# Half-K order for the last six output-projection chunks, with operand tiles reused for the block forms

## The chip, the cores and the metric

The kernel runs as one program on one core of a Trainium2 chip. The metric is the device time of one execution in microseconds (us), taken as the median of several runs. The engines are named as in the profile: PE (matmul), PEld (its weight loads), DVE (vector), ACT (scalar), POOL (GpSimd) and SP (which issues most DMAs).

## What is computed

One encoder layer in float32 on 512 tokens of width 2048. A mixing part (retention heads and state-space heads) ends in an output projection that is added to the residual; then come a gated MLP of inner width 5632 with a width-3 convolution on its gate, a gated per-layer input, and a last norm.

```python
h = h + jnp.concatenate([ret, ssd], axis=-1) @ w_out[i]
hn = rmsnorm(h, norm_ffn_w[i])
h = h + conv_glu_ffn(hn, ffn_w_gate[i], ffn_w_up[i], ffn_conv_w[i], ffn_conv_b[i], ffn_w_down[i])
gate = jax.nn.sigmoid(rmsnorm(h, ple_norm_w[i]) @ ple_w_gate[i] + ple_b_gate[i])
h = h + gate * (p[i] @ ple_w_proj[i])
return rmsnorm(h, final_norm_w)
```

## The kernel before, in words

Activations lie transposed: features on the 128 partitions, the 512 tokens along the row. A float32 product is made of three matmuls in the chip's fp32r type (`mm3`, L263): each operand is split into a high part (cast by ACT) and a low part (the rest, subtracted on DVE), and hi·hi, hi·lo and lo·hi are summed in PSUM. A weight unit is 128x1024 elements (512 KB), loaded by SP into one of four `raw` buffers and split into `whi` (L246, ACT) and `wlo` (L247, DVE), two units ahead of their use.

**Output projection** (L963 to 983). Sixteen chunks of 128 output features, in the order 0, 8, 1, 9, ... For each, `gemm_chunk` runs 16 steps of K with moving operands of 512 columns (`xh0..15`, `xl0..15`, the 64 KB pool `op` on the left side of SBUF). Then DVE adds the residual (`hc`, L969), ACT squares it for the norm (`sq`), POOL adds the squares up (`ssq`, L373), the chunk is stored to DRAM, and ACT writes it, times the norm weight, into `xw` (L978).

**MLP input** (L1009 to 1055, 44 chunks of the inner width). Gate and up projection are computed together by a seven-product block scheme. Input features pair up: chunk j with chunk j+8, eight pairs. For each pair there are seven operand forms of 256 tokens, high and low: `Eh{j}`, `El{j}` (`form_tiles`). Three forms are blocks of `xw` (`singles`), four are sums and differences of them (`sums`). A form costs DVE a subtraction for the low part (L932) and ACT a cast (L931), and the sums cost DVE five more adds of 256 columns per pair. One product (`prod`) runs over the eight pairs in the order j = 0 to 7, three matmuls of 256 columns each, 24 in all; a chunk has seven products, 168 matmuls. The weight forms are made the same way by `weight_form`.

Pairs 0 to 2 (`EARLY = 3`) are made during the output projection, in a pool on the right side. Pairs 3 to 7 lie in a pool on the left (`fb`) that takes the place of `op`; it opens only after the last output chunk, when `op` is closed. The norm (`token_norm`: 8 matmul records of one column, `rstd`, POOL's power, two diagonal tiles, two broadcast matmuls, copy into `Rb`) has its stages called in chunk 0 behind the first and second product, but a scheduler places instructions by priority and waits, so the order on each engine differs from the text.

**MLP output and gate.** Six groups of `acts` chunks, `ah`/`al`, lie alternately on the right (groups 0, 2, 4) and on the left (1, 3, 5) of SBUF. The per-layer gate uses sixteen operand pairs in `op2`, on the right. In the program as built, every operand tile on the right starts 32 bytes past a multiple of 64 bytes; the operand tiles of the same products on the left start on a multiple of 64.

Of the kernel before, what the change touches and what calls it, by code (L numbers as in the profile page):

```python
# [60 lines left out]
EARLY = 3  # L61
# [26 lines left out]
def layer(ctx: ExitStack, tc: tile.TileContext, xT, pT, pos, w_xbc, w_v, w_z, w_q, w_k, w_g,  # L88
# [11 lines left out]
    rope = mix.enter_context(tc.tile_pool(name="rope", bufs=1))  # L100
    ps = ctx.enter_context(tc.tile_pool(name="ps", bufs=4, space=PSUM))
# [227 lines left out]
    def diag_tokens(r, pool, tag=None):  # L329
# [4 lines left out]
        dh = pool.tile([P, NB, P], F32R, name=tag or "bc_dh", bufs=2 if tag else 1)[:, 0:nb]  # L334
        dl = pool.tile([P, NB, P], F32R, name=tag or "bc_dl", bufs=2 if tag else 1)[:, 0:nb]
# [620 lines left out]
    fa = ExitStack()  # L956
    fa_p = fa.enter_context(tc.tile_pool(name="fa", bufs=1, side="right", reuse_waits="tile"))
# [346 lines left out]
```

## Time and profile before

| what | us |
|---|---|
| median of 3 runs (2540.93 to 2545.3) | 2542.1 |
| the profiled execution, whole | 2543.66 |
| its span, first to last instruction | 2541.9 |
| PE busy in it | 2464.6 |
| mean granted clock of PE | 0.985 |

The profile has one execution. Its page shows busy time by engine, the span in 40 slices, the chain of work that ended last, the costliest groups of instructions and the DMA issues; the trace answers questions on a stretch, a line or a tile. Matmuls are pipelined: a record of a 512-column matmul lasts 0.39 us although the next starts 0.23 us later, so starts, not durations, are compared. 1.00 of granted clock is 2.4 GHz, 0.50 is 1.2 GHz.

### The profile page before, as it was taken

What the parts mean: (1) busy time and instruction counts of PE and PEld (TensorE: products, weight loads), DVE (VectorE), ACT (ScalarE), POOL (GpSimd) and SP (SyncE); (2) the same over time, 40 slices, a digit from 0 to 9 for tenths busy, and PEclk for the clock granted to TensorE, in tenths of its full rate; (3) what the DMA queues carried; (4) which work ended last, traced back from release to release, by engine and by line L of the source; (5) the groups of instructions that cost most, each with busy time, mean ns of one, the idle gap of its engine ahead of it and who ended that gap; (6) DMA issues with size and microseconds to landing.
All of it is one profiled execution on the core that took longest, in us unless ns stands there. A gap on an engine that the chain in (4) does not pass through costs nothing. (4 is left out here: it accounts for less than half of the span.)

```text
span 2541.9 us, 35008 instructions
## 1 busy us (share of the span) xinstructions
PE 2464.6 (97%) x14328; PEld 2165.9 (85%) x14328; DVE 1628.3 (64%) x1882; ACT 1005.2 (40%) x1374; POOL 257.4 (10%) x256
## 2 busy tenths in 40 slices
PE   8988899999999979999999999999999999999997
PEld 6867678888888869999999999999888888887886
DVE  7887552666555358888888888888744434346334
ACT  4333343444343335444444444444422212225342
POOL 6023210000002210000000000000210000002111
PEclk9999999999999979999999999999999999999998
DMA  5333323222234433333333333333454333322222
GB/s 192 110 92 99 108 76 106 89 90 91 80 116 149 141 99 115 120 113 113 119 122 125 121 113 113 121 121 127 152 178 133 124 98 126 104 92 91 96 95 83
DMA packets 100961, 289.29 MB, mean 114 GB/s; under 512 B 10656, under 2 KB 31392, under 8 KB 100800
## 3 DMA queue, kind: packets, MB, share of 16 engines
q1 hardware_dynamic: 91056, 255.58, 32.0%
q0 software_dynamic: 9600, 31.46, 3.4%
q8 instruction: 112, 1.84, 0.3%
q14 instruction: 49, 0.40, 0.0%
q10 hardware_dynamic: 144, 0.01, 0.0%
HBM read 267.02 MB, written 19.99 MB: 113 GB/s over the span
## 5 line engine op out<-in xcount | busy, mean ns | idle before, releaser
L247 DVE TENSOR_TENSOR wlo<-raw,whi 128x1024 fp32r<-128x1024 f32 (+1 forms) x395 | 492.5, 1248 | 444.6 <-ACT whi L246 444.3
L246 ACT CAST whi<-raw 128x1024 fp32r<-128x1024 f32 (+1 forms) x395 | 413.4, 1047 | 837.9 <-PE mm L265 712.9
L265 PE MATMUL mm<-El,whi 128*128 128x256 f32 x2464 | 700.9, 284 | 4.9 <-DVE El L932 4.9
L266 PE MATMUL mm<-Eh,wlo 128*128 128x256 f32 x2464 | 698.0, 283 | 0.8 <-DVE wlo L247 0.8
L264 PE MATMUL mm<-Eh,whi 128*128 128x256 f32 x2464 | 695.7, 282 | 3.0 <-ACT Eh L931 1.3
L265 PEld LDWEIGHTS mm<-El,whi 128*128 128x128 f32 x2464 | 471.5, 191 | 6.4 <-DVE El L932 6.3
L264 PEld LDWEIGHTS mm<-Eh,whi 128*128 128x128 f32 x2464 | 472.2, 192 | 4.5 <-ACT Eh L931 1.8
L266 PEld LDWEIGHTS mm<-Eh,wlo 128*128 128x128 f32 x2464 | 470.8, 191 | 1.1 <-DVE wlo L247 1.0
L264 PE MATMUL mm<-xh,whi 128*128 128x512 f32 (+1 forms) x1120 | 440.8, 394 | 6.3 <-ACT whi L246 5.1
L266 PE MATMUL mm<-xh,wlo 128*128 128x512 f32 (+1 forms) x1120 | 437.1, 390 | 3.2 <-DVE wlo L247 3.1
L265 PE MATMUL mm<-xl,whi 128*128 128x512 f32 (+1 forms) x1120 | 436.7, 390 | 2.0 <-DVE xl L295 2.0
L264 PE MATMUL mm<-ah,whi 128*128 128x512 f32 x704 | 275.3, 393 | 4.9 <-ACT ah L1073 4.9
L266 PE MATMUL mm<-ah,wlo 128*128 128x512 f32 x704 | 277.0, 394 | 0.0
L265 PE MATMUL mm<-al,whi 128*128 128x512 f32 x704 | 276.8, 393 | 0.0
L264 PEld LDWEIGHTS mm<-xh,whi 128*128 128x128 f32 x1120 | 211.8, 189 | 52.1 <-ACT whi L246 5.7
L265 PEld LDWEIGHTS mm<-xl,whi 128*128 128x128 f32 x1120 | 211.6, 189 | 51.1 <-DVE xl L295 5.5
L266 PEld LDWEIGHTS mm<-xh,wlo 128*128 128x128 f32 x1120 | 211.4, 189 | 49.0 <-DVE wlo L247 4.5
L246 ACT CAST whi<-rawB 128x1024 fp32r<-128x1024 f32 x132 | 138.6, 1050 | 175.8 <-PE mm L265 148.4
L247 DVE TENSOR_TENSOR wlo<-rawB,whi 128x1024 fp32r<-128x1024 f32 x132 | 161.2, 1222 | 45.3 <-ACT whi L246 45.3
L264 PEld LDWEIGHTS mm<-ah,whi 128*128 128x128 f32 x704 | 132.5, 189 | 35.5 <-ACT ah L1073 5.6
L265 PEld LDWEIGHTS mm<-al,whi 128*128 128x128 f32 x704 | 132.4, 188 | 31.4 <-DVE al L1074 0.6
L266 PEld LDWEIGHTS mm<-ah,wlo 128*128 128x128 f32 x704 | 132.4, 188 | 29.3
(274 smaller groups left out, 2561.1 us busy)
## 6 DMA issues: line engine op xcount, KB each, us to landing
raw<-in_w_down SPq DMA_DIRECT2D x88, 512.0 KB, 3.5
raw<-in_w_gate SPq DMA_DIRECT2D x44, 512.0 KB, 4.1
raw<-in_w_up SPq DMA_DIRECT2D x44, 512.0 KB, 5.0
rawB<-in_w_gate SPq DMA_DIRECT2D x44, 512.0 KB, 3.3
rawB<-in_w_up SPq DMA_DIRECT2D x44, 512.0 KB, 4.2
raw<-in_w_out SPq DMA_DIRECT2D x32, 512.0 KB, 3.6
raw<-in_w_ple SPq DMA_DIRECT2D x32, 512.0 KB, 3.5
raw<-in_w_xbc SPq DMA_DIRECT2D x25, 512.0 KB, 3.7
```

Source lines behind the costliest of these rows:

```text
L246: S.copy(hi[:, sl], r[:, sl])
L247: V.tensor_tensor(lo[:, sl], r[:, sl], hi[:, sl].bitcast(F32), op=ALU.subtract)
L264: TE.matmul(out, lh, rh, start=start, stop=False, skip_group_check=skip)
L265: TE.matmul(out, lh, rl, start=False, stop=False, skip_group_check=skip)
L266: TE.matmul(out, ll, rh, start=False, stop=stop, skip_group_check=skip)
```

## The change

The last six output chunks run the first half of K for all six, into six PSUM banks (four `mm`, two `mx`), and then the second half for each. The operands are now four tiles `X0` to `X3` of four chunks each. `X0` and `X1` (K steps 0 to 7) are free after the first halves, and the forms of pairs 4 and 5 are written into them; pairs 6 and 7 take `X2` and `X3`, which are free during and after the last half chunk. `EARLY` becomes 4, so pairs 0 to 3 are made on the right. The norm's diagonal tiles go into what is left over of `X0` and `X1`, and its stages are called later in chunk 0. The residual is loaded straight into `hc` (three buffers) and added in place. Pool `edge` pads the right side so that its tiles start on multiples of 64 bytes. Several small tiles move to the pool `rope`; `cc` has one buffer instead of two and `acc` two instead of three.

```diff
-EARLY = 3
+EARLY = 4
...
+    edge = ctx.enter_context(tc.tile_pool(name="edge", bufs=1, side="right"))
+    edge.tile([P, 8], F32, name="edge")
...
-    for n in OUT_ORDER:
+    TAIL = OUT_ORDER[-6:]
+    for n in OUT_ORDER[:-6]:
         add_chunk(w_out, n)
+    for u in range(2):
+        for n in TAIL:
+            units.append(w_out[n, :, 1024 * u:1024 * (u + 1)])
...
     def operands(c, src, wcol):
-        hi = op.tile([P, T], F32R, name=f"xh{c}")
-        lo = op.tile([P, T], F32R, name=f"xl{c}")
+        if c % 4 == 0:
+            quad[c // 4] = op.tile([P, 8 * T], F32R, name=f"X{c // 4}").rearrange("p (c n) -> p c n", n=T)
+        hi, lo = quad[c // 4][:, 2 * (c % 4)], quad[c // 4][:, 2 * (c % 4) + 1]
...
+    def form_tiles(j):
+
+        if j < EARLY:
+            E[j] = tuple(fa_p.tile([P, 7, HT], F32R, name=f"E{x}{j}") for x in "hl")
+        else:
+            t = op.tile([P, 8 * T], F32R, name=f"X{j - EARLY}")
+            E[j] = tuple(t[:, 7 * HT * i:7 * HT * (i + 1)].rearrange("p (s n) -> p s n", n=HT) for i in range(2))
+            room[j - EARLY] = t[:, 14 * HT:16 * HT].rearrange("p (b n) -> p b n", n=P)
...
+    edge2 = g1.enter_context(tc.tile_pool(name="edge2", bufs=1, side="right"))
+    edge2.tile([P, 496], F32, name="edge2")
+    fa_p = g1.enter_context(tc.tile_pool(name="fa", bufs=1, side="right", reuse_waits="tile"))
...
+    def out_done(i, n, bank):
+        j = i // 2
+        if i % 2 == 0:
+            xw[j] = late_p.tile([P, 4, HT], F32, name="xw", bufs=4)
+        hc = late_p.tile([P, T], F32, name="hc", bufs=3)
+        nc.sync.dma_start(hc, xT_v[n])
         with tc.high_priority():
-            V.tensor_tensor(hc, bank, xc, op=ALU.add)
+            V.tensor_tensor(hc, bank, hc, op=ALU.add)
...
+    for i, n in enumerate(OUT_ORDER[:-6]):
+        out_done(i, n, gemm_chunk(mops))
+        if i % 2 and i // 2 < EARLY:
+            forms(i // 2)
+
+    banks = [mm_bank() for _ in range(4)] + [mx_bank() for _ in range(2)]
+    for bank in banks:
+        half_chunk(bank, mops, 0)
+    forms(EARLY)
+    for i, n in enumerate(TAIL):
+        half_chunk(banks[i], mops, 1)
+        out_done(10 + i, n, banks[i])
+        if i == 1:
+            forms(EARLY + 1)
+
+
+    rest = range(EARLY + 2, KP)
+    for j in rest:
+        form_tiles(j)
+        singles(j)
...
+    norm_stages = token_norm(ss, None, into=room)
...
-        cc = m1.tile([P, HT], F32, name="cc", bufs=2)
+        cc = m1.tile([P, HT], F32, name="cc", bufs=1)
...
-        if c == 0:
-            norm_stages[0]()
-        prod(p, SLOT[1], True, True)
-        if c == 0:
-            norm_stages[1]()
...
+        prod(p, SLOT[1], True, True)
+        if c == 0:
+            norm_stages[0]()
...
+        if c == 0:
+            norm_stages[1]()
         V.tensor_tensor(up, up, Rb, op=ALU.mult)
...
-        acc = m1.tile([P, T], F32, name="acc", bufs=3)
+        acc = m1.tile([P, T], F32, name="acc", bufs=2)
```

What moves on the engines is shown at two places. The first is DVE around the residual add of the last output chunk. Before, from that add on (L969 is the add, L326 to L339 the norm, L219 and L228 weight sums, L247 a weight split, L932 the low part of a form):

```order
L969 TENSOR_TENSOR hc_6520<-mm_6463,xc_6461 128x512
L326 TENSOR_SCALAR rstd_t_6650<-mx_6645 128x4
L337 CAST bc_rh_6653<-rcol_83 128x4
L339 TENSOR_TENSOR bc_rl_6654<-rcol_83,bc_rh_6653 128x4
L219 TENSOR_TENSOR wsum_6615<-raw_6327,raw_6333 128x1024
L932 TENSOR_TENSOR El3_6533<-xw3_5895,Eh3_6532 128x256
L228 TENSOR_TENSOR raw_6329<-wsum_6615,raw_6329 128x1024
L932 TENSOR_TENSOR El3_6533<-xw3_5895,Eh3_6532 128x512
L247 TENSOR_TENSOR wlo_6618<-wsum_6615,whi_6617 128x1024
L932 TENSOR_TENSOR El4_6535<-xw4_6036,Eh4_6534 128x256
L932 TENSOR_TENSOR El4_6535<-xw4_6036,Eh4_6534 128x512
L932 TENSOR_TENSOR El5_6537<-xw5_6177,Eh5_6536 128x256
```

With the change, around the same add (now L994; L953 is the low part of a form, L968 to L974 the sums, L254 a weight split; `X2_6509` holds pair 6, `X3_6514` pair 7):

```order
L953 TENSOR_TENSOR X2_6509<-xw_6391,X2_6509 128x256
L953 TENSOR_TENSOR X2_6509<-xw_6391,X2_6509 128x512
L953 TENSOR_TENSOR X2_6509<-es_6519,X2_6509 128x512
L973 TENSOR_TENSOR xw_6391<-xw_6391 128x256
L994 TENSOR_TENSOR hc_6501<-mx_6071,hc_6501 128x512
L254 TENSOR_TENSOR wlo_6552<-wsum_6549,whi_6551 128x1024
L953 TENSOR_TENSOR X3_6514<-xw_6464,X3_6514 128x256
L968 TENSOR_TENSOR es_6524<-xw_6464 128x256
L974 TENSOR_TENSOR xw_6391<-xw_6391 128x256
L953 TENSOR_TENSOR X3_6514<-xw_6464,X3_6514 128x512
L969 TENSOR_TENSOR es_6524<-es_6524,xw_6464 128x256
L254 TENSOR_TENSOR wlo_6592<-raw_6271,whi_6591 128x1024
```

Before, all the forms of pairs 3 to 7 stand behind the last add; with the change most of pair 6 stands ahead of it and of the forms only pair 7 and one form of pair 6 are left.

The second place is PE where the norm is spread over the partitions, in chunk 0. Before (L347 and L348 are the two broadcast matmuls):

```order
L264 MATMUL mm_6613<-Eh7_6540,whi_6661 128x256
L265 MATMUL mm_6613<-El7_6541,whi_6661 128x256
L266 MATMUL mm_6613<-Eh7_6540,wlo_6662 128x256
L347 MATMUL mx_6689<-es_6655,ones_r_78 128x512
L348 MATMUL mx_6689<-es_6656,ones_r_78 128x512
L264 MATMUL mm_6612<-Eh0_5496,whi_6617 128x256
L265 MATMUL mm_6612<-El0_5497,whi_6617 128x256
```

With the change (L360 is the first of the two; the second now stands ahead of the last product of the chunk):

```order
L271 MATMUL mm_6547<-X3_6514,whi_6591 128x256
L272 MATMUL mm_6547<-X3_6514,whi_6591 128x256
L273 MATMUL mm_6547<-X3_6514,wlo_6592 128x256
L360 MATMUL mx_6755<-X0_6252,ones_r_82 128x512
L271 MATMUL mm_6546<-Eh0_5446,whi_6551 128x256
L272 MATMUL mm_6546<-El0_5447,whi_6551 128x256
L273 MATMUL mm_6546<-Eh0_5446,wlo_6552 128x256
```

In both, three products of chunk 0 are complete by then and four stand behind; now only one of the broadcasts is in that place.

## Rows read from the trace of the kernel before

**Rows 1.** The page: span, busy time by engine, PE and its granted clock by slice.
```profile
span 2541.9 us, 35008 instructions
...
PE 2464.6 (97%) x14328; PEld 2165.9 (85%) x14328; DVE 1628.3 (64%) x1882; ACT 1005.2 (40%) x1374; POOL 257.4 (10%) x256
...
PE   8988899999999979999999999999999999999997
...
PEclk9999999999999979999999999999999999999998
```

**Rows 2.** Busy time by stretch: PE, PEld, DVE, ACT, POOL, then PEclk, DMA share, GB/s.
```profile
913.60:961.20 47.60, 32.60 (x180) 28.49 (x179) 31.47 (x57) 19.60 (x33) 2.88 (x3) 0.68 0.28 94
961.20:981.40 20.20, 20.20 (x170) 20.06 (x169) 17.91 (x20) 10.96 (x14) 0.60 (x1) 1.00 0.34 118
981.40:1001.50 20.10, 20.10 (x171) 20.10 (x170) 17.56 (x20) 9.89 (x13) 0.54 (x1) 1.00 0.37 118
```

**Rows 3.** Busy time by shorter stretches, columns as in rows 2.
```profile
938.00:946.00 8.00, 2.27 (x4) 1.08 (x4) 7.73 (x16) 2.80 (x4) 0.00 (x0) 0.50 0.21 67
946.00:952.00 6.00, 5.05 (x24) 4.94 (x24) 0.04 (x1) 1.14 (x3) 0.00 (x0) 0.50 0.77 258
```

**Rows 4.** Who PE waited for, 913 to 962 us (total, times, longest).
```profile
PE mm L265 <- DVE El L932: 4.9, 5, 2.9
PE mx L347 <- DVE es L338: 4.8, 1, 4.8
```

**Rows 5.** Timeline, 913.6 to 952 us (start, duration).
```profile
913.64 0.28 PE L264 MATMUL mm<-Eh,whi 128*128 128x256 f32 x1
...
913.84 0.69 DVE L969 TENSOR_TENSOR hc<-mm,xc 128x512 f32<-128x512 f32 x1 [3.31 <-PE mm L266]
...
916.75 1.05 PE L320 MATMUL mx<-ones,ssq 128*128 128x1 f32 x8 [0.79 <-POOL ssq L373]
...
919.15 0.17 DVE L337 CAST bc_rh<-rcol 128x4 fp32r<-128x4 f32 x1 [1.15 <-POOL rcol L327]
...
943.78 0.80 PE L347 MATMUL mx<-es,ones_r 128*128 128x512 f32 x1 [4.77 <-DVE es L338]
```

**Rows 6.** L264 in MLP-output group 1, operands on the left.
```profile
L264 PE MATMUL mm<-ah,whi x128: 387/389/390, 1920.9 to 2007.3; 128*128 128x512 f32 x128
```

**Rows 7.** L264 in MLP-output group 2, operands on the right.
```profile
L264 PE MATMUL mm<-ah,whi x128: 392/392/397, 2008.0 to 2096.9; 128*128 128x512 f32 x128
```

**Rows 8.** L264 in four chunks of the per-layer gate, operands on the right.
```profile
L264 PE MATMUL mm<-xh,whi x64: 392/392/398, 2376.9 to 2421.0; 128*128 128x512 f32 x64
```

**Rows 9.** Instructions by line and shape, 840 to 960 us (count, busy us, mean ns).
```profile
L247 DVE TENSOR_TENSOR wlo<-wsum,whi 128x1024 fp32r<-128x1024 f32 x1 | 1.2, 1220 | 0.0
...
L932 DVE TENSOR_TENSOR El<-xw,Eh 128x512 fp32r<-128x512 f32 x10 | 6.9, 686 | 0.1
...
L217 DVE TENSOR_TENSOR raw<-raw 128x1024 f32<-128x1024 f32 x1 | 2.2, 2197 | 0.0
L932 DVE TENSOR_TENSOR El<-xw,Eh 128x256 fp32r<-128x256 f32 x5 | 2.1, 421 | 0.0
...
L931 ACT CAST Eh<-xw 128x256 fp32r<-128x256 f32 x5 | 2.0, 398 | 0.0
```

**Rows 10.** DMA issues of the page: KB each, median us to landing.
```profile
raw<-in_w_up SPq DMA_DIRECT2D x44, 512.0 KB, 5.0
...
xc<-in_xT SPq DMA_DIRECT2D x16, 256.0 KB, 2.9
h_d<-hc POOLq DMA_DIRECT2D x16, 256.0 KB, 3.2
```

**Rows 11.** Timeline of PE in one product: pair 0, pair 4, next product.
```profile
1001.49 0.28 PE L264 MATMUL mm<-Eh,whi 128*128 128x256 f32 x1
...
1002.91 0.28 PE L264 MATMUL mm<-Eh,whi 128*128 128x256 f32 x1
...
1004.36 0.28 PE L264 MATMUL mm<-Eh,whi 128*128 128x256 f32 x1
```

**Rows 12.** Tile acc, 1000 to 1100 us: first touch, store, its landing.
```profile
L1048 ACT ACTIVATE acc<-s,vec x5: 811/811/812, 1008.3 to 1088.5; 128x512 f32<-128x512 f32 x5
...
L1055 POOL DMA_DIRECT2D acts_d<-acc x5: 542/542/542, 1013.4 to 1093.7; - x5
...
DMA to landing us min/median/max: 3.1/3.5/5.1
```

**Rows 13.** Tile cc, 1000 to 1100 us: its copy and its one reader.
```profile
L1034 ACT COPY cc<-mm x5: 366/366/366, 1014.0 to 1094.3; 128x256 f32<-128x256 f32 x5
L1037 DVE TENSOR_TENSOR s<-cc,mm x5: 421/421/421, 1016.1 to 1096.4; 128x256 f32<-128x256 f32 x5
```

More of the change, by code (lines that the diff above doesn't have):

```diff
@@ L333, in diag_tokens @@
         rl = smalls.tile([P, NB], F32, name="bc_rl", bufs=2)[:, 0:nb]
[L334 to L335 removed]
+        if into:
+            dh, dl = into[0], into[1]
+        else:
+            dh = pool.tile([P, NB, P], F32R, name="bc_dh")[:, 0:nb]
+            dl = pool.tile([P, NB, P], F32R, name="bc_dl")[:, 0:nb]
         idb = ident.unsqueeze(1).broadcast_to([P, nb, P])
@@ L356, in layer, with __init__ @@
     class SumSq:
-        def __init__(self, pool, name="ssq", bufs=2):
+        def __init__(self, pool, name="ssq", bufs=2, acc_pool=None):
             self.pool, self.name, self.bufs, self.acc = pool, name, bufs, None
+            self.acc_pool = acc_pool or pool
         def add(self, src, on_pool=False):
             if self.acc is None:
-                self.acc = sq = self.pool.tile([P, src.shape[-1]], F32, name=self.name)
+                self.acc = sq = self.acc_pool.tile([P, src.shape[-1]], F32, name=self.name)
             else:
@@ L954, in sums @@
             form_split(j, 5, 2, xw[j][:, 1:3])
-    fa = ExitStack()
-    fa_p = fa.enter_context(tc.tile_pool(name="fa", bufs=1, side="right", reuse_waits="tile"))
+    g1 = ExitStack()
+    edge2 = g1.enter_context(tc.tile_pool(name="edge2", bufs=1, side="right"))
+    edge2.tile([P, 496], F32, name="edge2")
+    fa_p = g1.enter_context(tc.tile_pool(name="fa", bufs=1, side="right", reuse_waits="tile"))
+    gu_pool[1] = fa_p
+    ssq_p = g1.enter_context(tc.tile_pool(name="ssqp", bufs=1, side="right", reuse_waits="tile"))
@@ L978, in layer @@
-        S.activation(xw[j][:, 2 * (i % 2):2 * (i % 2) + 2], hc, AF.Copy, scale=vcol("norm_ffn", n))
-        if i % 2 and j < EARLY:
-            form_tiles(j, fa_p)
-            singles(j)
-            sums(j, 0)
-            sums(j, 1)
-    ox.close()
-    opx.close()
-    g1 = ExitStack()
-    fb_p = g1.enter_context(tc.tile_pool(name="fb", bufs=1, reuse_waits="tile"))
-    gu_pool[1] = fb_p
-    for j in range(EARLY, KP):
-        form_tiles(j, fb_p)
-    for j in range(EARLY, KP):
+        S.activation(xw[j][:, 2 * (i % 2):2 * (i % 2) + 2], hc, AF.Copy, scale=vcol("norm_ffn", n))
@@ L994, in layer, with forms @@
+    def forms(j):
+        form_tiles(j)
         singles(j)
-    for j in range(EARLY, KP):
         sums(j, 0)
-    for j in range(EARLY, KP):
         sums(j, 1)
-    norm_stages = token_norm(ss, late_p, tag="es")
-    m1 = None
+    for i, n in enumerate(OUT_ORDER[:-6]):
[5 more added lines that the diff above has]
+        half_chunk(bank, mops, 0)
@@ new lines, in layer @@
+    forms(EARLY)
[6 more added lines that the diff above has]
+    for j in rest:
+        form_tiles(j)
+        singles(j)
+    for j in rest:
+        sums(j, 0)
+    for j in rest:
+        sums(j, 1)
+    late.close()
+    m1 = g1.enter_context(tc.tile_pool(name="m1", bufs=1, side="right", reuse_waits="tile"))
+    gu_pool[0] = g1.enter_context(tc.tile_pool(name="w1", bufs=1, side="right", reuse_waits="tile"))
```

50 lines of the change are left out of this document (17 added, 33 removed).

## The prediction

> **What bounds the kernel now.** I read the page first. PE is busy for 2464.6 of 2541.9 us; DVE comes next with 64% [rows 1]. So a microsecond counts only where PE stands still, or where its matmuls come further apart than they need. The slices of PE and of its granted clock dip together in the fifteenth slice (890 to 953 us), and nowhere else from the sixth slice to the last but one [rows 1]. That is the step from the output projection to the MLP.
>
> The busy time by stretch gives that dip its size. Chunk 0 of the MLP runs from 913.6 to 961.2 us, 47.6 us; chunks 1 and 2, with the same 168 matmuls, take 20.2 and 20.1 us [rows 2]. PE is busy for 32.6 us of chunk 0 at a mean granted clock of 0.68 [rows 2]. From 938 to 946 us it has four instructions in 8 us while DVE is busy for 7.73; from 946 to 952 us it is busy again, but at 0.50, that is 1.2 GHz, after having been mostly idle [rows 3]. So some 27.5 us are lost, part as idle time and part at the low clock.
>
> The waits say for what: the low parts of the forms, 4.9 us, and the norm's first diagonal tile, 4.8 us [rows 4]. In the timeline that tile's source `bc_rh` is ready at 919.3, but the broadcast starts at 943.8 [rows 5], because DVE does the forms of five pairs in between. DVE bounds this stretch: 31.5 us of work in 47.6 [rows 2].
>
> The third view is the distance of matmul starts. In MLP-output group 1 (left) the 128 rows of L264 span 86.4 us, 127 steps of three matmuls: 226.8 ns each [rows 6]. In group 2 (right) they span 88.9 us: 233.3 ns [rows 7]. The per-layer gate (right): 44.1 us in 63 steps, 233.3 ns [rows 8]. Clock and work are the same. The right-side tiles start 32 bytes off a multiple of 64, the left ones on one; the trace doesn't tell side from offset.
>
> **The change, part by part.** *Forms, removed from the stall.* With t = 0 at the first MLP matmul, the last add starts at 0.2, as before [rows 5]. Ahead of it DVE has three low parts of pair 6 and one add: 0.42 + 0.69 + 0.69 + 0.42 = 2.2 us [rows 9]. They need `X2`, free after the first 12 of the 24 matmuls of the last half chunk, 12 x 0.227 = 2.7 us before t = 0; with a cast of 0.40 ahead [rows 9] they end near -0.1. Then come the last add 0.69, a weight split 1.22 and pair 7's first low part 0.42 [rows 9]: done near 2.5 to 2.6. PE works through pairs 0 to 6 until 21 x 0.12 = 2.5. So product 1 waits about 0.3 us. GpSimd's add of squares runs at that time: one DVE add of this shape lasted 2.20 us [rows 9] against about 1.22 for others of its size, so I allow 1.5 as the bound. The Trainium skill ("SBUF — State Buffer", Who interferes with whom) says that a DVE instruction with two SBUF inputs contends with a GpSimd one that reads SBUF; the long row agrees, and by the rule the wait would be nearer its bound.
>
> Pair 7's other forms end by about 8, each ahead of its product; products 2 and 3 (2.9 us each) do not wait.
>
> *Norm, moved later.* Its 8 records take 1.05 us [rows 5], from about 6 on. Before, from their start to the end of `bc_rh` took 2.6 us [rows 5]; the diagonal tile adds 0.69, so 3.3 us with DVE free, and up to 1.8 more behind a weight split and an add. PE has only one product of 2.9 us behind the 1.05 to cover it, so it waits up to 1.2 us at about 10, say 1.5 with the latencies; bounds 0 and 4. The two broadcasts cost 2 x 0.23. Whether the clock falls, I can't tell: I add 1.0, half of the 2 us that a few half-speed microseconds would cost; bounds 0 and 5. Chunk 0: 20.16 + 1.05 + 0.45 + 0.3 + 1.5 + 1.0 = 24.5. Against 47.5 that is **-23.0 us**; with the bounds -26 to -14.
>
> *Halves of K.* The matmuls are the same in number and shape; six banks hold the partial sums while no other work wants `mx`. Nothing.
>
> *SP and POOL.* A residual load now waits for the store of the chunk three earlier, and weight loads queue behind it on SP. Add, store (3.2 us) and load (2.9 us) [rows 10] take 7 us; in the tail three half chunks are 3 x 24 x 0.227 = 16.3 us. A weight load held back by about 4 us still has its 5.0 us [rows 10] before its unit, two and more half chunks of 5.4 us later. Hidden; if not, the same chunk shows an SP wait of a few us.
>
> *Padding, 512 columns.* Groups 0, 2 and 4 have 3 x 384 = 1152 matmuls, the gate 15 x 48 = 720 full ones. If the offset is the cause, each loses 6.5 ns: 1152 x 6.5 = **-7.5** and 720 x 6.5 = **-4.7**. If the side is the cause, 0.
>
> *Padding, 256 columns.* Here the rows speak against the change. In one product pairs 0 to 3 take 1.42 us and pairs 4 to 7 take 1.45 for 12 matmuls each [rows 11]; pairs 0 to 2 are the offset ones. With starts rounded to 0.01 and 2.867 us per product (20.07 / 7; the stores of `acc` are 80.3 us apart in four steps [rows 12]), I take 1.427 and 1.440: 120.0 ns when all is on 64, so a chunk takes 168 x 0.120 = 20.16 instead of 20.07. Over 43 chunks **+4.0**. The bounds are 1.42 and 1.45 for all: -8 and +10; the pairs with no offset neighbour are the nearest rows.
>
> Smaller tiles moved to `rope` and the in-place residual add: nothing, the same instructions off PE's path.
>
> Sum: -23.0 - 7.5 - 4.7 + 4.0 = -31.2. The profiled execution took 2543.7, so 2512.5; it lies 1.6 above the median of the runs, 2542.1, so **2511 us**.
>
> **The rivals.**
> 1. *Padding buys nothing* (the change does not do what it says). Then -23.0 alone: 2519. Against it: two stages on the right have the same 233.3 [rows 7, 8]. For it: side and offset are not told apart. The Trainium skill ("SBUF — State Buffer", Door 1: The DMA port swizzle) gives SBUF lines of 16 bytes with a penalty for each crossing; 32 bytes off is still on such a line, so by that rule this rival holds. What the trace shows for it stops at the confounded pair of rows.
> 2. *The stall stays in part.* DVE still has pair 7, the weight splits and the norm after t = 0, some 12 instructions ahead of the diagonal tile. If these or a late weight keep PE waiting 10 us in chunk 0, part of it at 0.50, the time is 2511 + 10 = 2521. For it: the forms of pair 7 depend on the last chunk; against: the walk above leaves 2 us of waits.
> 3. *Slower: the single `cc` and the two `acc` buffers.* If each of 43 chunks waited for one of them on PE, the saving of 31 us would be gone from 31 / 43 = 0.73 us per chunk on; with 1 us per chunk 2511 + 43 = 2554. Against it: the store of `acc` is issued at 1013.4 and lands within 5.1 us, and a buffer used every second chunk is written next at 1008.3 + 2 x 20.07 = 1048.4 [rows 12]; `cc` is read at 1016.1 and copied next at 1014.0 + 20.07 = 1034.1 [rows 13]. That leaves 30 and 17 us.
>
> **How the numbers follow.** Forecast 0.72; padding buys nothing 0.11; the stall stays in part 0.10; buffers, slower, 0.03; the rest 0.04, mostly faster still, by a gain at 256 columns. A measurement of this kernel can tell about 0.2%, 5 us, from no change. All cases but the buffers and some mishap lie beyond that: faster 0.95, within 0.02, slower 0.03. The forecast's own range is 2505 to 2518 (chunk 0 from 22 to 30 us, 256 columns a little either way); taking in rivals 1 and 2 gives 2503 to 2522.
>
> **What would show it.** Chunk 0 of the MLP should take 22 to 27 us with a clock near 1, its longest PE wait being for the diagonal tile. L264 in all MLP-output groups and in the gate should be 226.8 ns apart, and the later MLP chunks take 20.16 us. I am wrong in the main point if chunk 0 takes over 30 us, wrong on padding if groups 0, 2 and 4 still run at 233 ns, and wrong on its price if chunks keep 20.07 or go beyond 20.3.

## The result, and the profile after

| | us |
|---|---|
| before, median of 4 runs beside the change | 2542.9 |
| the change, median of 4 runs (2501.68 to 2509.38) | 2505.3 |
| ratio, 95% interval | 0.9852 [0.9837, 0.9867] |
| forecast (range) | 2511 (2503 to 2522) |
| the profiled execution of the change, whole | 2504.4 |
| its span (before 2541.9) | 2502.6 |

The total came out 6 us below the forecast and inside the range. Two of its parts missed by more than that. The page of the changed kernel, beside [rows 1], has no dip in the fifteenth slice of PE any more:

```profile
span 2502.6 us, 35014 instructions
...
PE 2437.6 (97%) x14328; PEld 2142.9 (86%) x14328; DVE 1631.4 (65%) x1882; ACT 1010.2 (40%) x1374; POOL 260.2 (10%) x256
...
PE   8989899999999999999999999999999999999997
...
PEclk9989899999999999999999999999999999999998
```

Busy time by stretch (us; PE, PEld, DVE, ACT, POOL, then PEclk, DMA share, GB/s). The first three stretches are chunks 0, 1 and 2 and answer to [rows 2]; the last two are the part of chunk 0 with the low clock and answer to [rows 3]:

```profile
912.90:940.90 28.00, 23.57 (x181) 22.62 (x180) 20.74 (x32) 12.24 (x18) 2.97 (x3) 0.94 0.47 161
940.90:960.60 19.70, 19.70 (x170) 19.62 (x169) 17.84 (x20) 11.07 (x14) 0.60 (x1) 1.00 0.35 121
960.60:980.20 19.60, 19.60 (x171) 19.60 (x169) 17.18 (x19) 9.89 (x13) 0.54 (x1) 1.00 0.40 121
...
918.00:920.00 2.00, 1.23 (x5) 1.24 (x6) 2.00 (x5) 0.77 (x2) 0.43 (x1) 0.56 0.11 43
920.00:922.00 2.00, 2.00 (x12) 2.00 (x12) 1.85 (x3) 1.47 (x3) 0.00 (x0) 0.59 0.03 8
```

Chunk 0 takes 27.9 us by its matmul starts (before 47.5), at a mean clock of 0.94 (before 0.68). The low clock is down to one piece, 918.2 to 921.7 us, which begins near the end of PE's idle time (915.7 to 918.8). But chunks 1 and 2 are shorter too, and so are all others. ACT's gelu comes once in each chunk, and 41 of them in 784.0 us make 40 steps of 19.60 us, where the prediction had 20.07 before and 20.16 after:

```profile
L1081 ACT ACTIVATE acc<-acc x41: 622/623/625, 970.2 to 1754.2; 128x512 f32<-128x512 f32 x41
```

Who PE waited for in chunks 0 and 1 (us in total, times, longest); this answers to [rows 4]:

```profile
PE mm L272 <- DVE X L953: 3.1, 1, 3.1
PE mx L360 <- DVE X L351: 1.0, 1, 1.0
PE mm L271 <- ACT ab L1051: 0.3, 1, 0.3
```

The longest wait is not the diagonal tile (1.0, L351) but pair 7's low part in product 1 (3.1, L953). Why it is late stands in the timeline (start, duration, engine), which answers to [rows 5]:

```profile
910.87 1.40 POOL L387 TENSOR_TENSOR ssq<-ssq,sq 128x512 f32<-128x512 f32 x1
911.04 1.52 DVE L972 TENSOR_TENSOR xw<-xw 128x256 f32<-128x256 f32 x1
912.48 1.21 DVE L235 TENSOR_TENSOR raw<-wsum,raw 128x1024 f32<-128x1024 f32 x1
913.62 1.01 DVE L953 TENSOR_TENSOR X<-xw,X 128x256 fp32r<-128x256 f32 x2
914.55 0.68 DVE L953 TENSOR_TENSOR X<-es,X 128x512 fp32r<-128x512 f32 x1
...
915.49 0.68 DVE L994 TENSOR_TENSOR hc<-mx,hc 128x512 f32<-128x512 f32 x1
916.09 1.21 DVE L254 TENSOR_TENSOR wlo<-wsum,whi 128x1024 fp32r<-128x1024 f32 x1
917.05 1.38 POOL L387 TENSOR_TENSOR ssq<-ssq,sq 128x512 f32<-128x512 f32 x1
917.23 1.48 DVE L953 TENSOR_TENSOR X<-xw,X 128x256 fp32r<-128x256 f32 x1
...
923.12 0.95 PE L330 MATMUL mx<-ones,ssq 128*128 128x1 f32 x8
```

The last residual add (`hc`, L994) starts at 915.49, 2.7 us after the first MLP matmul (912.80); the prediction had 0.2. Ahead of it DVE still works on pair 6 and on a weight sum (L235). Two of its instructions of 256 columns, L972 and the awaited L953, take 1.52 and 1.48 us while POOL adds squares; those of that shape with no POOL add beside them take 0.41 to 0.43. L972 and this L953 begin while POOL's add is under way and end 0.3 us after it. The weight split at 916.09 was under way when POOL's add began, and kept its 1.21 us. So what decides here is which of the two starts first.

Matmul rows of L271 in an MLP-output group on the left, in one on the right, and in four chunks of the gate (min/median/max ns of a record, first and last start); these answer to [rows 6 to 8]:

```profile
L271 PE MATMUL mm<-ah,whi x127: 389/389/395, 1882.3 to 1968.0; 128*128 128x512 f32 x127
...
L271 PE MATMUL mm<-ah,whi x128: 392/394/398, 1968.6 to 2057.5; 128*128 128x512 f32 x128
...
L271 PE MATMUL mm<-X,whi x63: 392/392/398, 2338.2 to 2381.6; 128*128 128x512 f32 x63
```

Left: 85.7 us in 126 steps of three, 226.7 ns. Right: 88.9 us in 127 steps, 233.3 ns. Gate: 43.4 us in 62 steps, 233.3 ns. The padding changed nothing here, although the right side's operands now start on a multiple of 64 bytes.

By spans the 39.3 us come from chunk 0 (-19.6) and from chunks 1 to 42 (-0.5, then 41 times -0.467, -19.6 in all); everything else sums to nothing.

### The profile page after: what moved, and what is told of

Same layout as the page of the kernel before. It is cut to its first block, busy times and chain, and to the rows that moved or that the text cites. A ratio compares the mean times of both kernels' runs of the same rounds, so it can differ in the third digit from the quotient of the medians.

```text
span 2502.6 us, 35014 instructions
## 1 busy us (share of the span) xinstructions
PE 2437.6 (97%) x14328; PEld 2142.9 (86%) x14328; DVE 1631.4 (65%) x1882; ACT 1010.2 (40%) x1374; POOL 260.2 (10%) x256
## 5 line engine op out<-in xcount | busy, mean ns | idle before, releaser
L271 PE MATMUL mm<-X,whi 128*128 128x256 f32 (+1 forms) x2320 | 775.6, 334 | 5.6 <-ACT whi L253 5.1
L272 PE MATMUL mm<-X,whi 128*128 128x256 f32 (+1 forms) x2320 | 770.1, 332 | 5.0 <-DVE X L953 3.1
L273 PE MATMUL mm<-X,wlo 128*128 128x256 f32 (+1 forms) x2320 | 770.8, 332 | 3.2 <-DVE wlo L254 3.2
L254 DVE TENSOR_TENSOR wlo<-raw,whi 128x1024 fp32r<-128x1024 f32 (+1 forms) x395 | 491.9, 1246 | 430.8 <-ACT whi L253 428.3
L272 PEld LDWEIGHTS mm<-X,whi 128*128 128x128 f32 x2320 | 438.4, 189 | 52.5 <-DVE X L305 5.4
L271 PEld LDWEIGHTS mm<-X,whi 128*128 128x128 f32 x2320 | 438.8, 189 | 50.1 <-ACT whi L253 5.6
L273 PEld LDWEIGHTS mm<-X,wlo 128*128 128x128 f32 x2320 | 438.6, 189 | 47.8 <-DVE wlo L254 4.6
L271 PE MATMUL mm<-Eh,whi 128*128 128x256 f32 x1232 | 344.2, 279 | 0.4 <-ACT ab L1051 0.3
L272 PE MATMUL mm<-El,whi 128*128 128x256 f32 x1232 | 342.6, 278 | 0.0
L273 PE MATMUL mm<-Eh,wlo 128*128 128x256 f32 x1232 | 341.6, 277 | 0.0
L271 PE MATMUL mm<-ah,whi 128*128 128x512 f32 x704 | 276.5, 395 | 5.7 <-ACT ah L1101 5.7
L271 PEld LDWEIGHTS mm<-Eh,whi 128*128 128x128 f32 x1232 | 233.0, 189 | 0.9 <-ACT ab L1051 0.6
L272 PEld LDWEIGHTS mm<-El,whi 128*128 128x128 f32 x1232 | 233.1, 189 | 0.1
L273 PEld LDWEIGHTS mm<-Eh,wlo 128*128 128x128 f32 x1232 | 232.3, 189 | 0.1
L254 DVE TENSOR_TENSOR wlo<-rawB,whi 128x1024 fp32r<-128x1024 f32 x132 | 161.4, 1223 | 36.1 <-ACT whi L253 33.9
L271 PEld LDWEIGHTS mm<-ah,whi 128*128 128x128 f32 x704 | 133.1, 189 | 35.9 <-ACT ah L1101 5.9
```

What stands on the lines that cost most here:

```text
L254: V.tensor_tensor(lo[:, sl], r[:, sl], hi[:, sl].bitcast(F32), op=ALU.subtract)
L271: TE.matmul(out, lh, rh, start=start, stop=False, skip_group_check=skip)
L272: TE.matmul(out, lh, rl, start=False, stop=False, skip_group_check=skip)
L273: TE.matmul(out, ll, rh, start=False, stop=stop, skip_group_check=skip)
```

## The experiments

Two questions: what spaces the matmuls, and which part of the new order shortened chunk 0. All times are medians beside runs of the kernel before (2543.6 to 2544.0). Distances between matmul starts are means from the trace's own starts, which the lines shown round to 0.1 us.

### Rows of matmuls by themselves (m1_offsets)

The layer is left out: 48 matmuls into one bank per row, one execution, with the moving and the weight operand at chosen places.

```diff
+    for n, m, wo, high in CONFIGS:
+        bank = ps.tile([P, T], F32, name="mm")
+        for r in range(REPS):
+            a = (HIGH if high else 0) + m // 4 + 512 * (r % 4)
+            b = wo // 4 + P * (r % 8)
+            TE.matmul(bank[:, 0:n], w[:, b:b + P], big[:, a:a + n], start=(r == 0), stop=(r == REPS - 1))
```

> Leaves out the whole layer: it only runs rows of 48 fp32r matmuls (512 or 256 columns, a weight load for each) whose moving operand starts at a chosen byte offset of a 2048-byte line of SBUF, low or high in the partition, with the weights at a chosen offset too; the distance of starts is the result. Theory A, the place in a line of 1024 or 2048 bytes sets the distance: 256 columns about 113 ns at offset 0 and 1024 and 118 to 120 elsewhere; 512 columns about 220 ns at offset 0, 226.7 at most offsets and 233.3 at 1984 and 2016, the same low and high. Theory B, a multiple of 64 bytes is what counts: 226.7 and 120 at all offsets but 32, 992 and 2016, which are slower by 6 to 7 ns. Theory C, the side counts: the same at all offsets low, 6 to 7 ns more at all offsets high.

Four rows of it: 512 columns with the weights at 64 and the moving operand at 0, then with the weights at 128 and the moving operand at 1920 bytes; the same two for 256 columns (columns as in the rows above):

```profile
L41 PE MATMUL mm<-big,w x44: 393/396/398, 326.6 to 336.6; 128*128 128x512 f32 x44
L41 PE MATMUL mm<-big,w x44: 389/389/389, 371.0 to 380.8; 128*128 128x512 f32 x44
L41 PE MATMUL mm<-big,w x44: 276/276/277, 476.1 to 481.0; 128*128 128x256 f32 x44
L41 PE MATMUL mm<-big,w x45: 278/283/283, 498.5 to 503.7; 128*128 128x256 f32 x45
```

No theory of the expectation holds. Low and high addresses give the same, and starts on multiples of 64 differ among themselves. What orders the rows is the **distance** from the weight operand's start to the moving operand's start, modulo 256 bytes, that is, what is left of it after division by 256 (theory D from here on):

| distance | 512 columns, ns | 256 columns, ns |
|---|---|---|
| 0 | 226.7 | 120.0 |
| 64 | 228.9 | 117.8 |
| 128 | 232.2 to 233.4 | 118.7 |
| 192 | 233.3 | 113.3 |

Moving the weights instead gives the same table: weights 64 and moving 0 (distance 192) 233.4 and 113.3; weights 128 and moving 1920 (distance 0) 226.7 and 120.0. Read back into the kernels by their addresses: before, the weight tiles stand at 128 modulo 256, the left operands at 128 (distance 0), the right ones at 224 (distance 96). After, the weights stand at 64 and the MLP-output operands on the right at 192, distance 128. The padding moved them from one slow distance to another. The block operands on the right went to distance 192, the best one for 256 columns.

The table is for rows of one distance; a product that mixes distances does not follow it matmul by matmul. In the later chunks of the change pairs 1 to 3 (distance 192) run at 113.3 to 113.6 ns, but pair 0, at the same distance and behind pair 7, at 119.5, and pairs 4 to 7 (distance 0) at 116.1, 119.4, 118.0 and 120.0.

### The order without the second pad, without both, and the pads alone

e1_no_edge2 takes `edge2` out of the change; e2_no_pads takes out both; e3_pads_alone puts both into the kernel before.

```diff
-    edge = ctx.enter_context(tc.tile_pool(name="edge", bufs=1, side="right"))
-    edge.tile([P, 8], F32, name="edge")
...
-    edge2 = g1.enter_context(tc.tile_pool(name="edge2", bufs=1, side="right"))
-    edge2.tile([P, 496], F32, name="edge2")
```

> The changed kernel without the second pad of 1984 bytes, so that the forms on the right start at 1984 of a 2048-byte line (still on 64). Theory A: MLP chunks go from 19.60 back to 20.0 to 20.2 us, 44 x 0.5 = about 22 us slower than the changed kernel, 2525 to 2530. Theory B: 19.60 us a chunk, 2505. MLP output groups 0, 2, 4 and the gate stay at 233 ns under both.

> The changed kernel without either pad: right-side tiles 32 bytes off a multiple of 64 again; the order of work is that of the change. Theory A: like the run without the second pad alone, MLP chunks near 20.07 us, 2523 to 2530, so the 64-byte pad itself is worth under 3 us. Theory B: 6 us or more slower than without the second pad alone. Both: chunk 0 stays near 28 us, so about 20 us under the kernel before is the order's share.

> The kernel before with both pads and nothing else of the change. Theory A: pairs 0 to 2 on the right now start on multiples of 1024 and their matmuls come near 113 ns apart; MLP chunks about 19.8 us, 44 x 0.27 = 12 us faster than before, 2531; chunk 0 still 47 us; groups 0, 2, 4 and the gate stay at 233 ns. Theory B: the gain is in groups 0, 2, 4 and the gate, 12 us, and MLP chunks are 20.16.

The line of the gelus of e2, and one of an MLP-output group on the right of e3:

```profile
L1077 ACT ACTIVATE acc<-acc x41: 619/623/627, 970.2 to 1763.5; 128x512 f32<-128x512 f32 x41
...
L266 PE MATMUL mm<-ah,whi x128: 394/394/397, 2004.8 to 2092.1; 128*128 128x512 f32 x128
```

The first is 793.3 us in 40 steps, 19.83 us a chunk; the second 228.9 ns a matmul. Neither theory of the expectations holds: e1 and e2 lie 6 and 7 us under theory A's ranges, and theory B wanted 2505 for e1, e2 slower than e1, and chunks of 20.16 us in e3.

| kernel | median us | ratio to before | chunk 0 | later chunks | distance of the blocks on the right |
|---|---|---|---|---|---|
| before | 2544.0 | 1 | 47.5 | 20.067 | 96 (3 pairs) |
| e3, pads alone | 2534.4 | 0.9966 [0.9953, 0.9979] | 46.7 | 20.067 | 128 (3 pairs) |
| e2, order alone | 2515.6 | 0.9890 [0.9875, 0.9905] | 26.8 | 19.833 | 160 (4 pairs) |
| e1, order and `edge` | 2519.4 | 0.9908 [0.9891, 0.9925] | 29.4 | 19.973 | 128 (4 pairs) |
| the change | 2505.3 | 0.9852 [0.9837, 0.9867] | 27.9 | 19.600 | 192 (4 pairs) |

So the order, with the layout that it brings, is worth 28.4 us, and the pads 10.3 on top of it, nearly all by the later chunks (42 x 0.233 = 9.8). `edge` alone costs 3.8 us. In the kernel before the same pads put the MLP output's right groups and the gate at distance 64, where they run at 228.9 instead of 233.3 ns; (1152 + 720) x 4.4 = 8.2 of the 9.6 us gained. The pads help, then, but by which distance they leave, and not by the multiple of 64 that `edge` makes. Chunk 0 itself moves between 26.8 and 29.4 us with the layout alone; differences of some 2 us there should not be read as an effect of an order.

### The starts set by theory D (f1_zero_512, f2_192_blocks)

f1 changes only where the right side's tiles begin:

```diff
-    edge2.tile([P, 496], F32, name="edge2")
+    edge2.tile([P, 48], F32, name="edge2")
...
+    edge3 = ctx.enter_context(tc.tile_pool(name="edge3", bufs=1, side="right"))
+    edge3.tile([P, 32], F32, name="edge3")
     open_group(0)
```

> The changed kernel with only the right side's starts moved: the pad beside the blocks is 48 elements instead of 496, and a pad of 32 elements is put ahead of the activations of the MLP output. By their addresses the blocks keep their distance from the weight tiles (192 bytes modulo 256), and the 512-column operands of the MLP output's right groups and of the gate go from 128 to 0. Theory D (the distance between the moving and the weight operand's starts, modulo 256 bytes, sets the matmul's start distance): all MLP-output groups and the gate at 226.7 ns; some 1,150 + 720 matmuls times 6.6 ns make 12.4 us, so about 2493 (2490 to 2496), chunks of the MLP unchanged at 19.60. Rival (the side of the memory sets it, as the prediction's rival had it): 233.3 ns stays in groups 0, 2, 4 and the gate, 2505.

f2 also shifts the blocks that replace used operands:

```diff
-            t = op.tile([P, 8 * T], F32R, name=f"X{j - EARLY}")
+            t = op.tile([P, 8 * T], F32R, name=f"X{j - EARLY}")[:, 48:]
...
+    for i in range(2):
+        room[i] = m1.tile([P, T], F32R, name="acc", bufs=2).rearrange("p (b n) -> p b n", n=P)
     norm_stages = token_norm(ss, None, into=room)
```

> As the run before (moving starts of the 512-column operands at distance 0), and the block operands that replace the used ones are shifted by 48 elements inside their tiles, so that they too lie 192 bytes (modulo 256) past the weight operand; the norm's two diagonal tiles move from the tiles' spare end into the two buffers of acc. Theory D: pairs 4 to 7 go from 116 to 120 ns to the 113.3 ns of pairs 1 to 3; 3,696 matmuls times about 5 ns make 18 us, chunks about 19.2 us, whole about 2475 (2470 to 2480). Rival (it is the place on the right side that makes pairs 1 to 3 fast): chunks stay at 19.60 and the whole at the time of the run before.

f1: 2492.7 us, ratio 0.9799 [0.9781, 0.9816], 12.6 us less than the change where 12.4 were expected. A left group, a right group and the gate in its trace:

```profile
L271 PE MATMUL mm<-ah,whi x128: 389/389/389, 1881.2 to 1967.6; 128*128 128x512 f32 x128
...
L271 PE MATMUL mm<-ah,whi x128: 389/389/389, 1968.2 to 2054.6; 128*128 128x512 f32 x128
...
L271 PE MATMUL mm<-X,whi x63: 389/389/389, 2331.7 to 2373.8; 128*128 128x512 f32 x63
```

All three now come 226.7 ns apart (86.4 us in 127 steps of three, 42.1 in 62), on the right as on the left. Side is out, and theory D holds for 512 columns.

f2: median 2471.5 us, ratio 0.9742 [0.9679, 0.9806], but its four executions are 2500.57, 2473.69, 2467.86 and 2469.34. The long one is the profiled one. Its gelus:

```profile
L1082 ACT ACTIVATE acc<-acc x41: 622/627/628, 971.2 to 1762.7; 128x512 f32<-128x512 f32 x41
```

791.5 us in 40 steps, 19.79 us a chunk: here every pair is at 117.8 ns, pairs 1 to 3 too, which had 113.3 to 113.6 in f1. The other executions are 26.9 to 32.7 us shorter; (2500.57 - 2469.34) / 43 = 0.73 us a chunk, which would make 19.06, or 113.4 ns a matmul. So the distance alone doesn't set the time at 192 bytes: it looks as if there were two rhythms, that is, two steady spacings of the same matmuls.

### Two rhythms (m2_rows, f3_pair0_at_64)

Each row of m2 is a list of distances:

```diff
+ROWS = [(n, [r] * 48) for n in (512, 256) for r in range(0, 256, 16)]
+ROWS += [(256, [a] * 24 + [Z] * 72) for a in (0, 32, 64, 128)]
+ROWS += [(256, [Z] * 24 + [a] * 3 + [Z] * 69) for a in (0, 32, 64, 128)]
...
+ROWS += [(256, ([64] * 3 + [Z] * 21) * 4), (256, ([128] * 3 + [Z] * 21) * 4)]
+ROWS += [(256, [Z] * 96)] * 4
```

> The layer is left out: rows of matmuls in one bank, each with its moving operand at a chosen distance from its weight operand. 32 rows go through 0 to 240 bytes in steps of 16, for 512 and 256 columns; 13 rows of 96 matmuls of 256 columns mix distances; four rows are 96 matmuls at 192 bytes. Theory D (the distance alone sets it): 226.7 ns at 0 and 228 to 234 elsewhere for 512 columns, 113.3 ns at 192 and 117 to 120 elsewhere for 256, and in the mixed rows the 192-byte part at 113.3 whatever went before. Theory M (at 192 bytes there are two rhythms, 113.3 and 117.8, and what went before chooses; the profiled run of f2 kept 117.8 in all 43 later chunks where its other runs were some 30 us shorter): some of the mixed rows, or of the four equal ones, stay at 117.8.

Rows of 256 columns, most of each row: (1) 24 matmuls at 128, then 72 at 192; (2) 24 at 192, three at 0, 69 at 192; (3) four times three at 64 and 21 at 192; (4) 192 throughout:

```profile
L43 PE MATMUL mm<-big,w x93: 279/281/285, 310.9 to 321.8; 128*128 128x256 f32 x93
L43 PE MATMUL mm<-big,w x92: 278/281/283, 322.3 to 333.0; 128*128 128x256 f32 x92
L43 PE MATMUL mm<-big,w x92: 276/276/280, 399.6 to 410.0; 128*128 128x256 f32 x92
L43 PE MATMUL mm<-big,w x92: 276/276/276, 454.3 to 464.6; 128*128 128x256 f32 x92
```

Row 2 is at 117.8 ns throughout but for a mean of 118.2 around the three at 0 (10.7 us in 91 steps), row 4 at 113.3 (10.3 us in 91). Both are at 192. Row 1 settles at 117.8 and stays there for its last 72; a row that begins with 24 at 0, 32 or 64 falls to 113.3 within some eight matmuls. One row that began at 117.8 was brought to 113.3 by three matmuls at 32, where three at 0 (row 2) did not. In these rows, of one execution, theory M holds: two rhythms, chosen by what went before. Of the 16 distances, 512 columns have 226.7 only at 0 and 240 and 228.9 to 234.6 at the others (the first row, at 0, took 427 to 592 ns for each of its first twelve matmuls and reached 226.7 after them); 256 columns have 113.3 at 112 and 192 and 116.6 to 120.0 at the others. 64-byte steps are not special. Each is one row, and two of them differ from m1 at 256 columns: 116.6 against 117.8 at 32 bytes, 117.4 against 118.6 at 160. So 192 may not be the only distance with two rhythms.

f3 takes f2 and puts one pair of each product at 64, as in row 3, which averages 114.0:

```diff
-            E[j] = tuple(fa_p.tile([P, 7, HT], F32R, name=f"E{x}{j}") for x in "hl")
+            a = 0 if j else 32
+            E[j] = tuple(fa_p.tile([P, 7 * HT + 2 * a], F32R, name=f"E{x}{j}")[:, a:a + 7 * HT]
+                         .rearrange("p (s n) -> p s n", n=HT) for x in "hl")
```

> The kernel of f2 (every block operand 192 bytes past its weight operand), but pair 0's blocks are moved to a distance of 64 bytes, by 32 elements inside larger tiles. In the rows measured by themselves, three matmuls at 64 among 21 at 192 took 115.8 ns over the first eight and 113.4 over the others, 114.0 on average, in every repetition, while rows at 192 alone ran at 113.3 or at 117.8. Theory M with a way out (the one pair at 64 brings each product back to the faster rhythm): chunks 168 times 114.0 ns, 19.16 us, in every execution; whole 2505.3 less 12.5 for the 512-column matmuls (f1) less 44 times 0.44 us, that is 2473, and all executions within 6 us of it. Rival (the rhythm is chosen elsewhere and a pair at 64 does not undo it): some executions near 2500 with chunks of 19.79 us, the others near 2470, as in f2.

2475.1 us, ratio 0.9729 [0.9716, 0.9742]. Five executions lie between 2473.7 and 2476.2, at the 2473 expected, and the profiled one at 2500.7:

```profile
L1084 ACT ACTIVATE acc<-acc x41: 620/622/628, 971.5 to 1762.9; 128x512 f32<-128x512 f32 x41
```

791.4 us in 40 steps, 19.79 us a chunk again, pair 0 at 118.9 ns, pair 1 at 116.7, pairs 2 to 7 at 117.8. So the pair at 64 is no way out, and the rival's outcome is there as well. What chooses the rhythm in the whole kernel stays **open**: both long executions are the profiled ones, which are also the first of their kernel, and no run separates the two. That the eight others ran at the fast rhythm is inferred from their times; no trace shows it. Either way f2 and f3 beat the kernel before and the change, the latter by some 5 us in the long executions and by 29 to 37 in the others.

### The order, undone step by step (g1 to g4)

g1 puts the norm's stages back behind products 1 and 2. g2 lets the last six output chunks take all of K one after the other. g3 is g2 with the blocks' tiles in the opposite order (pair 4 takes `X3`, pair 7 `X0`), meant to leave no block to be made before the last matmul. g4 is g3 with g1's edit.

```diff
g1
+        if c == 0:
+            norm_stages[0]()
         prod(p, SLOT[1], True, True)
         if c == 0:
-            norm_stages[0]()
+            norm_stages[1]()
g2
-    for n in OUT_ORDER[:-6]:
+    for n in OUT_ORDER:
         add_chunk(w_out, n)
...
+    for i, n in enumerate(TAIL):
+        out_done(10 + i, n, gemm_chunk(mops))
-    rest = range(EARLY + 2, KP)
+    rest = range(EARLY, KP)
g3
-            t = op.tile([P, 8 * T], F32R, name=f"X{j - EARLY}")
+            t = op.tile([P, 8 * T], F32R, name=f"X{7 - j}")
```

> The changed kernel with only the norm's two stages put back where they were, behind products 1 and 2 of chunk 0. My theory (the later norm is worth a few us, because the sums of squares come 5 us into the chunk): the TensorE waits about 2.6 us for the sum after product 1 and some 3 to 5 us for the diagonal tiles after product 2, chunk 0 at 32 to 36 us instead of 27.9, whole 2509 to 2513. Rival (the waits only change place): chunk 0 within 1 us of 27.9, whole 2505. Later chunks unchanged at 19.60 by both.

> The changed kernel with the last six output chunks taking all of K one after the other, so that no used operand is free before the last of them and the blocks of pairs 4 to 7 are all made behind it; pads, four early pairs and the later norm stay. My theory (the two halves of K are what removes the stall, since they let pairs 4 and 5 be made beside TensorE work): of the former 27 us of stall four pairs' share less the norm's waits, so 15 to 20, comes back; chunk 0 at 36 to 42 us, whole 2515 to 2520. Rival (the fourth early pair and the later norm do it): chunk 0 at 28 to 31 us, whole 2505 to 2509. Later chunks unchanged at 19.60.

> The kernel of the run with all of K (g2), with one more thing undone: the blocks of pairs 4 to 7 take the used tiles in the opposite order (pair 4 the tile whose operands the last matmuls read), so that no block can be made before the last matmul of the output projection. Theory R (what is left of the gain in g2 comes from the release tile by tile, which lets the DVE start on pair 4 about 8 us before the last matmul ends): chunk 0 goes from 31.5 to 38 to 42 us, with more of it at the half clock; whole 2516 to 2520. Rival F (the fourth early pair and the later norm make the gain): chunk 0 within 1.5 us of 31.5, whole 2508 to 2511. Later chunks at 19.60 by both.

> The kernel of the run before (g3) with the norm's stages also back behind products 1 and 2: of the change's order only the fourth early pair and the operand tiles as blocks' home are left, and the pads. By the chain so far (the norm's place was worth 3.6 us in g1, and 5.5 us of waits stand at it in the kernel before): chunk 0 4 to 6 us above g3's. If theory R holds, that is 42 to 47 us, little under the 46.7 us of the kernel before with pads (which makes five pairs there, one pair is 4.5 us of DVE work); if F holds, 35 to 37 us, and the fourth pair made up the rest, some 10 us.

| kernel | what is undone | chunk 0, us | median us | ratio to before |
|---|---|---|---|---|
| the change | nothing | 27.9 | 2505.3 | 0.9852 [0.9837, 0.9867] |
| g1 | the norm's place | 31.6 | 2509.5 | 0.9867 [0.9851, 0.9882] |
| g2 | the halves of K | 31.5 | 2509.1 | 0.9869 [0.9851, 0.9887] |
| g3 | halves, order of the blocks' tiles | 33.9 | 2512.0 | 0.9879 [0.9862, 0.9895] |
| g4 | halves, order of the tiles, norm's place | 41.8 | 2519.3 | 0.9902 [0.9887, 0.9917] |
| e3 (before with the pads) | also the fourth early pair, the used tiles as the blocks' home and the rest | 46.7 | 2534.4 | 0.9966 [0.9953, 0.9979] |

Later chunks are at 19.60 in g1 to g4. PE's waits of g1, then g2, g3 and g4, around chunk 0:

```profile
PE mx L330 <- POOL ssq L387: 2.9, 1, 2.9
PE mx L360 <- DVE X L351: 1.8, 1, 1.8
PE mx L361 <- DVE X L353: 1.7, 1, 1.7
```

```profile
PE mm L268 <- ACT ab L1041: 5.6, 1, 5.6
PE mm L269 <- DVE X L950: 1.9, 2, 1.0
```

```profile
PE mx L357 <- DVE X L348: 6.5, 1, 6.5
PE mx L327 <- POOL ssq L384: 2.2, 1, 2.2
```

```profile
PE mx L357 <- DVE X L348: 6.5, 1, 6.5
PE mx L327 <- POOL ssq L384: 5.1, 1, 5.1
```

In g2 PE's longest wait, 5.6 us, is put down to ACT's copy of a product; in g3 and g4 it is the norm's diagonal tile again, 6.5 us, as in the kernel before with 4.8 [rows 4].

g3 does not do what it was meant to do. Its trace has DVE making low parts of blocks 6.4 us ahead of the first MLP matmul (912.55):

```profile
906.15 0.41 DVE L950 TENSOR_TENSOR X<-xw,X 128x256 fp32r<-128x256 f32 x1
...
909.89 0.41 DVE L950 TENSOR_TENSOR X<-xw,X 128x256 fp32r<-128x256 f32 x1
...
912.55 0.28 PE L268 MATMUL mm<-Eh,whi 128*128 128x256 f32 x1
```

By the tiles of the program these two are of pairs 7 and 6, which take `X0` and `X1`, the tiles that come free first. Five low parts begin ahead of the first MLP matmul in g3 and four in g2, the first 6.4 us ahead in both. So the release tile by tile was turned round, not undone, and theory R is untested.

In g4 the wait for the squares is one long POOL add:

```profile
918.02 1.22 DVE L251 TENSOR_TENSOR wlo<-wsum,whi 128x1024 fp32r<-128x1024 f32 x1
918.65 5.12 POOL L384 TENSOR_TENSOR ssq<-ssq,sq 128x512 f32<-128x512 f32 x1
...
922.23 0.42 DVE L965 TENSOR_TENSOR es<-xw 128x256 f32<-128x256 f32 x1
...
923.83 1.87 PE L327 MATMUL mx<-ones,ssq 128*128 128x1 f32 x8 [5.11 <-POOL ssq L384]
```

DVE was at work when the add began and ran on without a break until 922.65; the add took 5.12 us, where the same one takes 1.38 in the change and 2.34 in g2. In g3 it takes 6.26. This is the other direction of what held up pair 7 in the change: here POOL comes second.

My theory on the halves fell: without them chunk 0 takes 31.5 us, not 36 to 42. In g3 it takes 33.9, which neither theory R (38 to 42) nor rival F (30 to 33) had, and PE has a wait of 2.2 us for the squares that g2 does not have. The theory on the norm nearly held in g1 (31.6, just under 32 to 36); from g3 to g4 the norm's place moves chunk 0 by 7.9 us, more than the 4 to 6 expected. The chain of 18.8 us from e3 to the change is 4.9 for the fourth early pair with the used tiles as the blocks' home and the rest of the layout, 7.9 for the norm's place, 2.4 for the order of the tiles and 3.6 for the halves. The 4.9 is about the 4.5 us of DVE work of one pair, but what the release by itself is worth stays open. Each chunk 0 is that of one execution, and the 2.4 is no more than the layout alone can make (26.8 to 29.4 above). The order in which they are undone matters, since the norm is worth 3.6 in g1 and 7.9 in g4. In g4 the clock falls twice, at 921.3 us in the wait for the squares and at 938.4 in that for the diagonal tile: its chunk 0 has a mean clock of 0.76, g3's 0.90.

```profile
916.30:958.10 41.80, 28.67 (x181) 27.18 (x180) 23.41 (x42) 15.18 (x23) 7.12 (x3) 0.76 0.32 108
```

(g4, busy time by stretch, columns as above.) PE is busy for 28.67 us with what later takes 19.6, and idle for 13.1. In the kernel before the same figures are 32.60 busy and 15.0 idle, at 0.68 [rows 2].

## Why the prediction was right, and where it was wrong

Forecast 2511, measured 2505.3, faster as forecast. One term is right in mechanism and 3.4 us off in size; the two on padding are wrong, by +12.2 and -23.6 us. These errors sum to -8, the -39.3 of the spans against the -31.2 forecast. That the total came out so near is luck: its parts miss by more and cancel.

1. **Chunk 0, -23.0 forecast, -19.6 measured.** The reading of what bounds the kernel held. The mis-sized term is "product 1 waits about 0.3 us" (bound 1.5): it waits 3.1 us. The walk along DVE's queue took DVE as free 2.3 us ahead of the first MLP matmul. It was held by an add of pair 6 (L972, 1.52 us beside a POOL add) and a weight sum that the walk left out (1.21 us, L235), so pair 6's low parts began 0.8 us after that matmul; the `hc` add came at 2.7 us and not at 0.2, and pair 7's low part took 1.48 us beside the next POOL add. The Trainium skill ("SBUF — State Buffer", Who interferes with whom), cited in the prediction for the bound, agrees with 1.48 and 1.52 against 0.42, and it applied twice, not once. The wait (+2.8), the norm's wait (-0.5), the low clock (+0.7), a wait for ACT's copy (+0.3) and the faster matmuls (19.60 against 20.16) make 2.7 of the 3.4 us; the rest is not assigned. The upper bounds of the prediction add up to 32.2 us, a gain of 15 and not 14.
2. **The norm's wait, 1.5 forecast, 1.0 measured; the low clock, 1.0 forecast.** 3.4 us at 1.2 GHz cost about half of that, an estimate of 1.7. Both lie within their bounds. That the clock would fall behind the wait in product 1, and not behind the norm's, was not foreseen.
3. **Halves of K, SP and POOL at no cost: right for the halves and for SP.** PE waits for no weight load in chunk 0, and SP waits 1.6 us for stores of the residual sum from 880 to 945 us. POOL's add of squares was not free, see 1. The prediction gave chunk 0 one sum and did not split it between the early forms and the norm's place; in the order tried here the norm's place has the largest share of the chain (7.9 us, but 3.6 when it alone is undone).
4. **Padding, 512 columns, -7.5 and -4.7 forecast, 0 measured.** The step that failed is "If the offset is the cause, each loses 6.5 ns", with the offset taken modulo 64 bytes. Side is not the cause either, as f1 shows. In its place: the distance to the weight operand modulo 256, 96 before and 128 after, both at 233.3 ns. With the distance at 0 the gain is there, 12.6 us.
5. **Padding, 256 columns, +4.0 forecast, -19.6 measured.** The step that failed is "120.0 ns when all is on 64"; the bounds of -8 to +10 did not hold it. The small difference between pairs 0 to 3 and 4 to 7 [rows 11] was real, but it is not that of the offset pairs: over 40 chunks pairs 0 to 2, the offset ones, run at 119.4, 120.8 and 119.2 ns, pair 3, which has no offset, at 116.1 and pairs 4 to 7 at 120.0. The twelve matmuls of pairs 0 to 3 hid that. Half of the -19.6 came with the pads (19.833 to 19.600), half with the layout that the order brought by itself (20.067 to 19.833, e2), which the prediction did not consider.
6. **The rivals.** Rival 1 (padding buys nothing) holds for the stages it spoke of, and its total of 2519 fails by the later chunks. The rule that the prediction cites from the Trainium skill ("SBUF — State Buffer", Door 1: The DMA port swizzle) would make all starts on 16-byte lines alike; the 16 distances in steps of 16 run from 226.7 to 234.6 ns, so the rule doesn't account for the spacing. Rival 2 (some 10 us of waits left) did not come: waits of 4.4 us were left. Rival 3 (single `cc`, two `acc`) left no wait in any chunk; the later chunks repeat at 19.60.

## What to carry to other kernels

Where the same matmuls run at two spacings, compare the starts of both operands, the weights' as well as the moving one's, before naming a side or an alignment; here some bytes of padding were worth 10 to 13 us, while a pad to a multiple of 64 bytes (`edge`) cost 3.8 us by itself. A walk along a queue needs every instruction on it, those for the next stage's weights too, at the duration it has beside what POOL does at that time. When several edits remove one stall, undo them one at a time, and read in the trace that the edit did undo it: the halves of K were worth 3.6 us, the moved norm 3.6 to 7.9, and the edit meant to undo the early release did not.

## What the runs showed of the hardware

- The start-to-start time of matmuls with 512 columns is 226.7, 228.9, 232.2 to 233.4 and 233.3 ns at distances of 0, 64, 128 and 192 bytes (modulo 256) between the weight and the moving operand; with 256 columns the order is nearly reversed, 120.0, 117.8, 118.7 and 113.3, in rows of one distance.
- At 256 columns and 192 bytes two rhythms exist, 113.3 and 117.8 ns, and in rows by themselves the matmuls before choose. In a whole kernel the slower one held for all later chunks of a traced execution; other executions were 25 to 33 us shorter, about as the faster one would make them, but what chooses there is open.
- A DVE instruction of 256 columns with two inputs in SBUF took 0.42 us alone and 1.48 to 1.52 us when it began during a POOL add of 512 columns. Where DVE had begun first and ran on, the POOL add took 5.12 us (g4) and 6.26 us (g3) instead of 1.38 (the change).
